# A two-block transformer kernel: score tiles, TensorE taps, norm sums, mask selects, band bias and key projection rearranged

## The chip, the cores and the metric

One Trainium2 chip, one core of it. The metric is the device time in microseconds (us) of one execution of the whole kernel; the kernel before took 2129.66 us as the median of three runs (2129.12 to 2134.75).

## What is computed

`reference` runs two transformer blocks on one sequence of 512 tokens, width 1024, all in float32. The parts that the change touches, cut to what matters:

```python
# first block: sliding-window attention beside a convolution branch
proj = rms_norm(h, mix_pre_g) @ w_in              # q (8 heads x 64), k, v (2 heads), u (2 x 512)
s = einsum(q, k) * scale + bias_by_distance       # blocks of 128 queries, 256 keys, window 128
p = softmax with a sink term;  attn_out = p @ v
a, gate = split(u);  c = a * sigmoid(gate)
c = depthwise causal convolution of c, width 31, 512 channels
c = silu(layer_norm(c)) @ w_conv_pw
h = h + rms_norm(concat(attn_out, c) @ w_out)
h = h + rms_norm((silu(hn @ w_gate) * (hn @ w_up)) @ w_down)
# second block: spatial gating beside attention on selected keys, then a table of experts
z = tril(spatial_w) @ layer_norm(gelu(v));  y_a = gelu(u) * z
k = rope(rms_norm(c_n @ w_uk)); vv = c_n @ w_uv;  q = rope(rms_norm(q))
y_b = softmax over the 256 (or fewer) keys with the highest index scores
h = h + merge(y_a, y_b) @ w_o;  h = h + peer(rms_norm(h))
```

## The kernel before

**Arithmetic.** Tokens lie in four blocks of 128 (`tb`). Large products are split: each float32 operand becomes a high part (a cast on ScalarE, ACT) and a low part (a subtraction on VectorE, DVE), and `mm3` (L155 to L158) makes three matmuls of them on TensorE (PE). A weight unit (`unit`, L132) is one load of 128 x 1024 on SP's queue, a cast on ACT (L138) and a subtraction on DVE (L140), in a ring of four; `next_unit` takes the units in the order in which they are packed. Plain float32 matmuls (transposes, scores, taps, means) show two records each in the trace. PSUM has eight banks, four with the tag "a" and four with "b".

**Order.** The program is traced by Tile, which gives each engine its own queue: of what is ready by its own estimate it issues first what was traced first, so the order of the code is a priority and not the exact order of a queue. Each queue then runs strictly in order on the chip. Work on different streams is interleaved by generators: `advance(gen, us)` traces as much of a generator as the given budget covers, `zipped` alternates several and `chain` puts them one behind the other. `tc.issue_after(x)` (`order`) queues an instruction behind `x` on the same engine without waiting for its end.

**First block, attention and convolution (L332 to L543).** `conv(c, ...)` makes one of four channel groups: a gated input `hc`, a first tap on ACT (L358), then the other 30 taps as multiply-adds of 128x512 on DVE (L368), each reading and writing `acc[c]`. For groups 2 and 3 the first `N_PE_TAPS[c]` taps (12 and 8) are instead matmuls on PE against diagonal matrices (`pe_taps`, L363; the diagonals are made on ACT, L347), and one DVE addition (L364) joins their sum to `acc[c]`. L498 to L500 trace both `pe_taps` ahead of the DVE taps of groups 2 and 3. Before the projections of q, k and v (L417), L401 to L407 build the band bias: four transfers on POOL's queue that read a small DRAM tile in reversed rows (L403), four matmuls (L405), four DVE additions (L406). `att1(b)` (L428) is the attention of block b: score matmuls (L435) and their DVE evacuation (L439) into two score tiles `sa`, of which the pool has `SA_BUFS` = 4 in all; maxima on DVE (L446), exponentials and scaling on ACT (L455, L460), transposes (L466) and products with v (L469) on PE, and a split into `cathi`/`catlo` (L472). Blocks 0 and 1 run together, then 2 and 3 (`att23`, L478), which at its step 3 (counted from 0) also traces the first two units of the output projection for token blocks 0 and 1 (L482 to L484). Behind all of it come the mean over channels (L513), the rest of those two units (L515, L533) between the steps of the layer norm (L516 to L538), and the pointwise convolution (L539).

**Transitions (`transition`, L243).** Three times the kernel ends a projection, adds it to `h`, normalises and transposes. Per token block: squares with a sum on ACT for each half (L253, L293), an addition of the two sums on DVE (L281, L295), scale and epsilon on DVE (L163), the power -1/2 on POOL (L164), products on DVE (L284, L298), transposes on PE (L183). The first two transitions do this twice per block (norm of the result, norm for the next layer), the third once.

**Second block (L602 to L862).** Index scores, then a top-k on DVE (`topk`, L704: 16 rounds of maximum and replacement for each of blocks 1 to 3), traced in small steps between the projections, with the attention `att2` chained behind it. The query projection goes to four "a" banks (L725 to L727). Then, for each block, six short matmuls project keys and values into a "b" bank (L743 to L746); ACT copies the values (L747) and squares queries and keys (L751, L752), DVE normalises (L755, L757, reading both banks), rotates, and PE makes one more projection into a "b" bank (L760) and transposes (`turn`). Then come the value projections (L822), the layer norm of the gate, two gates (L840) and the spatial gate (L843 to L855), which reads `wsT`. Its lower triangle is kept by four selects on POOL (L815 to L817), with no order given but their place in the code. Eight more gate projections follow among the steps of `att2`.

## Time and profile before

| | |
|---|---|
| runs, us | 2129.12, 2129.66, 2134.75 (median 2129.66) |
| profiled execution, us | 2132.12 |
| its span in the profile, us | 2130.4 |
| mean granted TensorE clock | 0.988 of full |
| first block, attention and convolution | about 34 to 200 us of the span |
| first, second, third transition | about 200 to 255, 584 to 627, 900 to 945 us |
| second block up to its merge | about 627 to 820 us |
| experts | from about 945 us to the end |

How to read the profile: it shows one execution; busy times are per engine, and a wait is put down to what ended it. PE is the matmul part of TensorE, PEld its weight load. A granted clock of 1.00 is 2.4 GHz; TensorE runs at that or at 1.2 GHz, so a value between is a mixture over the stretch. A wait of a row stands in brackets at its end, with the engine, tile and line that ended it. `x40` is the number of records in a row.

### The profile page before, as it was taken

The page shows a single profiled execution, that of the slowest core. Times are in us where ns is not written, and L with a number is a line of the kernel's source. Part 1 is how long each engine was busy: PE and PEld are TensorE (multiplying, and loading weights), DVE is VectorE, ACT ScalarE, POOL GpSimd, SP SyncE. Part 2 cuts the span into 40 slices and gives each one's busy share as a digit, 9 for nine tenths or more (in the row PEclk, how much of TensorE's full clock was granted, in tenths as well). Part 3 has the DMA queues.
Part 4 walks back from the last instruction along what each step waited for, and adds up shares of the span by engine and source line. Part 5 has one row for each costly group of instructions (what it writes and reads, how often), then busy time and mean ns, then how long its engine had stood idle before and what let it go on. Part 6 is the DMA issues. An engine that isn't in the chain of part 4 may idle for free.

```text
span 2130.4 us, 29554 instructions
## 1 busy us (share of the span) xinstructions
PE 2061.1 (97%) x11128; PEld 1753.5 (82%) x11128; DVE 1573.1 (74%) x2901; ACT 825.7 (39%) x1339; POOL 520.2 (24%) x383
## 2 busy tenths in 40 slices
PE   7989999999989999999999999999999999999999
PEld 6746888888877877888889899999888878788887
DVE  6974633332268955455699999998999988899997
ACT  5354422221244342333453455555433333333332
POOL 1000000000010000000032222220575656566573
PEclk9998999999999999999999999999999999999999
DMA  5202232333222222333278889899999999999995
GB/s 188 82 28 69 72 107 93 95 99 117 84 87 80 70 89 69 109 124 98 81 288 278 289 299 358 290 365 307 390 394 411 389 402 387 410 402 411 411 399 223
DMA packets 163281, 476.47 MB, mean 224 GB/s; under 512 B 13865, under 2 KB 57265, under 8 KB 161218
## 3 DMA queue, kind: packets, MB, share of 16 engines
...
## 4 chain that ended last, share of the span: by engine, by line
PE 54%; DVE 21%; issue 13%; DMA 8%; POOL 3%; ACT 2%; DVEq 0%; POOLq 0%; SPq 0%; ACTq 0%
PE bank_a L156 12%; PE bank_a L157 12%; PE bank_a L158 12%; DVE wlo L140 5%; PE bank_b L156 4%; PE bank_b L157 4%; PE bank_b L158 4%; DMA rows<-in_peer_u_dram,gidx 2%; DVE rows L957 2%; POOL rows L941 2%; DMA rows<-in_peer_v_dram,gidx 2%; DMA al<-a_dram 2%; DVE h L964 2%; DVE rows L949 2%; PE bank_b L1108 1%
## 5 line engine op out<-in xcount | busy, mean ns | idle before, releaser
L138 ACT CAST whi<-raw 128x1024 fp32r<-128x1024 f32 (+1 forms) x413 | 431.9, 1047 | 884.0 <-PE bank_a L157 332.0
L140 DVE TENSOR_TENSOR wlo<-raw,whi 128x1024 fp32r<-128x1024 f32 (+1 forms) x413 | 499.9, 1213 | 265.9 <-ACT whi L138 263.6
L156 PE MATMUL bank_a<-xhi,whi 128*128 128x320 f32 (+2 forms) x1600 | 549.3, 344 | 0.8 <-ACT xhi L152 0.8
L158 PE MATMUL bank_a<-xhi,wlo 128*128 128x320 f32 (+2 forms) x1600 | 546.2, 342 | 3.3 <-DVE wlo L140 3.3
L157 PE MATMUL bank_a<-xlo,whi 128*128 128x320 f32 (+2 forms) x1600 | 548.0, 343 | 0.6 <-DVE xlo L153 0.6
L941 POOL DMA_INDIRECT rows<-in_peer_u_dram,gidx x192 | 279.0, 1453 | 553.4 <-DVE gidx L1042 143.1
L158 PEld LDWEIGHTS bank_a<-xhi,wlo 128*128 128x128 f32 x1600 | 303.5, 190 | 31.6 <-DVE wlo L140 5.3
L156 PEld LDWEIGHTS bank_a<-xhi,whi 128*128 128x128 f32 x1600 | 302.8, 190 | 28.3 <-ACT xhi L152 1.8
L157 PEld LDWEIGHTS bank_a<-xlo,whi 128*128 128x128 f32 x1600 | 303.7, 190 | 26.9 <-DVE xlo L153 1.6
L941 POOL DMA_INDIRECT rows<-in_peer_v_dram,gidx x128 | 206.2, 1611 | 115.2 <-DVE h L964 91.2
L164 POOL TENSOR_TENSOR rstd<-rstd,neghalf 128x1 f32<-128x1 f32 (+2 forms) x37 | 25.2, 682 | 844.2 <-DVE rstd L163 832.4
L156 PE MATMUL bank_a<-whi,wvhi 128*128 128x512 f32 x512 | 201.9, 394 | 7.4 <-ACT wvhi L152 7.3
L157 PE MATMUL bank_a<-wlo,wvhi 128*128 128x512 f32 x512 | 202.0, 394 | 1.7 <-DVE wlo L140 1.6
L158 PE MATMUL bank_a<-whi,wvlo 128*128 128x512 f32 x512 | 201.7, 394 | 1.7 <-DVE wvlo L153 1.6
L964 DVE SCALAR_TENSOR_TENSOR h<-rows,ga,h 128x1024 f32<-128x1024 f32 x128 | 164.1, 1282 | 5.6 <-DMA rows<-in_peer_v_dram,gidx 4.2
L957 DVE SCALAR_TENSOR_TENSOR rows<-rows,h 128x1024 f32<-128x1024 f32 x128 | 152.8, 1220 | 9.9 <-DMA rows<-in_peer_u_dram,gidx 9.9
L156 PEld LDWEIGHTS bank_a<-whi,wvhi 128*128 128x128 f32 x512 | 97.0, 189 | 28.7 <-ACT wvhi L152 9.1
L158 PEld LDWEIGHTS bank_a<-whi,wvlo 128*128 128x128 f32 x512 | 97.2, 190 | 24.9 <-DVE wvlo L153 4.2
L157 PEld LDWEIGHTS bank_a<-wlo,wvhi 128*128 128x128 f32 x512 | 97.0, 189 | 21.6 <-DVE wlo L140 2.4
L156 PE MATMUL bank_b<-whi,wvhi 128*128 128x512 f32 x256 | 99.9, 390 | 0.0
L158 PE MATMUL bank_b<-whi,wvlo 128*128 128x512 f32 x256 | 99.6, 389 | 0.0
L157 PE MATMUL bank_b<-wlo,wvhi 128*128 128x512 f32 x256 | 99.6, 389 | 0.0
(403 smaller groups left out, 3272.5 us busy)
## 6 DMA issues: line engine op xcount, KB each, us to landing
...
raw<-in_ut_dram SPq DMA_DIRECT2D x128, 512.0 KB, 5.8
raw<-in_peer_v_dram SPq DMA_DIRECT2D x128, 512.0 KB, 8.0
...
```

The source lines that it names most:

```text
L138: lead[0] = S.copy(hi[:, :n], raw[:, :n]).ins
L140: pace[0] = V.tensor_tensor(lo[:, :n], raw[:, :n], hi[:, :n].bitcast(F32), op=OP.subtract).ins
L156: T.matmul(o, lh, rh, start=start, stop=False)
L157: T.matmul(o, lh, rl, start=False, stop=False)
L158: T.matmul(o, ll, rh, start=False, stop=stop)
L164: G.tensor_tensor(r, r, neghalf[:, :shape[1]], op=OP.pow)
L941: G.indirect_dma_start(out=r, out_offset=None, in_=table, in_offset=bass.IndirectOffsetOnAxis(ap=idx[:, k:k + 1], axis=0))
L949: V.scalar_tensor_tensor(r, r, 1.0, hn2, op0=OP.mult, op1=OP.mult, accum_out=ga2[:, k:k + 1])
L957: V.scalar_tensor_tensor(r, r, 1.0, hn3, op0=OP.mult, op1=OP.mult, accum_out=ga[:, k:k + 1])
L964: V.scalar_tensor_tensor(h[3], r, ga[:, k:k + 1], h[3], op0=OP.mult, op1=OP.add)
L1108: T.matmul(gp[:, j, :], o_[:, g2, :, t2], oh1[:, g2, :, t2], start=o_ is ohs[0], stop=o_ is ohs[-1])
```

## The change

Seven edits:

- `N_PE_TAPS` becomes (0, 0, 8, 8): four taps of group 2 go from PE to DVE, and four diagonals are no longer made. `SA_BUFS` becomes 7.
- The two `pe_taps` are traced inside `att23`, at its steps 4 and 6 (counted from 0), when all scores of blocks 2 and 3 are traced; the DVE taps of groups 2 and 3 that the budget has reached by then are traced ahead of them.
- The output projection's first two units are traced for all four token blocks behind the mean, one ahead of the variance and one behind the matmul that spreads the reciprocal root.
- The band bias is made in a function that is called behind projections 1 to 4 of the six.
- In the transitions, squares are scaled by 1/32 inside the activation, so that `rsqrt2` can add the two sums and epsilon in one DVE instruction.
- The key and value projection of block j is traced behind step j of the query projection, with the keys copied to SBUF on ACT (`ksb`), and the later steps read the copy.
- The four selects on `wsT` are issued behind the last power on POOL traced so far, that of the key norms.

```diff
--- before.py
+++ after.py
@@ -28,9 +28,9 @@
 GATHER = 0.5
 G_US = 2.3
 NSPILL = 100
-N_PE_TAPS = (0, 0, 12, 8)
+N_PE_TAPS = (0, 0, 8, 8)
 N_GATE = 5
-SA_BUFS = 4
+SA_BUFS = 7
 CONV_US = 4.4
 ATT_US = 2.0
 ATT2_US = 1.0
@@ -157,11 +157,20 @@
         T.matmul(o, lh, rl, start=False, stop=False)
         T.matmul(o, ll, rh, start=False, stop=stop)
 
+    rooted = [None]
+
     def rsqrt(ssq, scale, shape, after=None):
         r = small.tile(shape, F32, name="rstd", tag=f"rstd{shape[1]}")
         with order(after):
             V.tensor_scalar(r, ssq, scale, EPS, op0=OP.mult, op1=OP.add)
-        G.tensor_tensor(r, r, neghalf[:, :shape[1]], op=OP.pow)
+        rooted[0] = G.tensor_tensor(r, r, neghalf[:, :shape[1]], op=OP.pow).ins
+        return r
+
+    def rsqrt2(ssq):
+
+        r = small.tile([128, 1], F32, name="rstd", tag="rstd1")
+        V.tensor_scalar(r, ssq[:, 0:1], ssq[:, 1:2], EPS, op0=OP.add, op1=OP.add)
+        rooted[0] = G.tensor_tensor(r, r, neghalf[:, 0:1], op=OP.pow).ins
         return r
 
     def norm(wk, src, g_b, xs=None, after=(None, None)):
@@ -250,7 +259,7 @@
         ssq = [small.tile([128, 2], F32, name=f"ssqo{tb}", bufs=2) for tb in range(4)]
 
         def sumsq(o, tb, hf):
-            S.activation(xhi[:, tb, 4 * hf:4 * hf + 4, :], o.rearrange("p (k t) -> p k t", k=4), AF.Square,
+            S.activation(xhi[:, tb, 4 * hf:4 * hf + 4, :], o.rearrange("p (k t) -> p k t", k=4), AF.Square, scale=1.0 / 32,
                          accum_out=ssq[tb][:, hf:hf + 1])
 
         os0, j0 = pre or ([bank("a") for _ in range(4)], 0)
@@ -277,9 +286,7 @@
             if gp is not None:
                 sumsq(os1[tb], tb, 1)
                 V.tensor_tensor(xs[:, 512:], os1[tb], g_post[:, 512:], op=OP.mult)
-                s1 = small.tile([128, 1], F32, name="ssq1")
-                V.tensor_tensor(s1, ssq[tb][:, 0:1], ssq[tb][:, 1:2], op=OP.add)
-                r = rsqrt(s1, 1.0 / 1024, [128, 1])
+                r = rsqrt2(ssq[tb])
                 for sl in halves:
                     V.scalar_tensor_tensor(h[tb][:, sl], xs[:, sl], r, h[tb][:, sl], op0=OP.mult, op1=OP.add)
             else:
@@ -290,10 +297,8 @@
 
             sq = small.tile([128, 2], F32, name="ssqn", bufs=2)
             for hf, sl in enumerate(halves):
-                S.activation(xs[:, sl], h[tb][:, sl], AF.Square, accum_out=sq[:, hf:hf + 1])
-            s1 = small.tile([128, 1], F32, name="ssq1")
-            V.tensor_tensor(s1, sq[:, 0:1], sq[:, 1:2], op=OP.add)
-            r = rsqrt(s1, 1.0 / 1024, [128, 1])
+                S.activation(xs[:, sl], h[tb][:, sl], AF.Square, scale=1.0 / 32, accum_out=sq[:, hf:hf + 1])
+            r = rsqrt2(sq)
             for sl in halves:
                 V.scalar_tensor_tensor(xs[:, sl], h[tb][:, sl], r, g_next[:, sl], op0=OP.mult, op1=OP.mult)
             last = xs
@@ -398,16 +403,14 @@
         bap = bdr[:, :]
         band = cst1[:, 0:256]
         flip = cst1[:, 256:384]
-        for j in range(4):
+
+        def band_bias(j):
             rev = pt_.tile([128, 2, 256], F32, name="rev", bufs=2)
             nc.gpsimd.dma_start(rev, bass.AP(tensor=bap.tensor, offset=bap.offset + 2 * j * 383, ap=[[1, 128], [383, 2], [1, 256]]))
             fp = bank("b")
             T.matmul(fp, flip, rev.rearrange("p a k -> p (a k)"), start=True, stop=True)
             V.tensor_tensor(bias[:, 2 * j:2 * j + 2, :], fp.rearrange("p (a k) -> p a k", a=2),
                             band[:, None, :].to_broadcast([128, 2, 256]), op=OP.add)
-
-        stt.close()
-        at = pool("b1at", stack=st, side="right")
 
 
         qT = pa.tile([128, 4, 512], F32, name="qT")
@@ -418,7 +421,11 @@
             S.copy(dst, proj_T(next_unit(), xhi, xlo))
             if n_ in (0, 1):
                 diagonals(2 + n_)
+            if 1 <= n_ <= 4:
+                band_bias(n_ - 1)
             d = advance(cv, d + CONV_US)
+        stt.close()
+        at = pool("b1at", stack=st, side="right")
         vps = bank("b")
         for b in range(4):
             T.transpose(vps[:, b * 128:(b + 1) * 128], vT[:, b * 128:(b + 1) * 128], ident)
@@ -472,21 +479,17 @@
             split(cathi[:, b, 0:4, :], catlo[:, b, 0:4, :], op_.rearrange("p (c t) -> p c t", c=4))
             yield 0.7
 
-        os0, us0 = [], []
-        src1 = (lambda tb, k: cathi[:, tb, k, :]), (lambda tb, k: catlo[:, tb, k, :])
+        c23 = []
 
         def att23():
 
             for n_, t in enumerate(zipped(att1(2), att1(3))):
-                if n_ == 3:
-                    us0.extend(next_unit() for _ in range(2))
-                    os0.extend(bank("a") for _ in range(2))
-                    proj_tok(os0, *src1, range(2), 8, 0, us0, 2, 512)
+                if n_ in (4, 6):
+                    c23[n_ // 2 - 2][1]()
                 yield t
 
         av = chain(zipped(att1(0), att1(1)), att23())
         da = 0.0
-        c23 = []
         for c in (2, 3):
             oa = proj_T(next_unit(), xhi, xlo)
             d = advance(cv, d + CONV_US)
@@ -495,11 +498,7 @@
             c23.append(conv(c, oa, og))
             d = advance(cv, d + CONV_US)
             da = advance(av, da + ATT_US)
-        for c in (0, 1):
-            c23[c][1]()
-            da = advance(av, da + ATT_US)
-        c23 = [c_[0] for c_ in c23]
-        cv = chain(cv, zipped(*c23))
+        cv = chain(cv, zipped(*[c_[0] for c_ in c23]))
         while True:
             n1 = next(cv, None)
             da = advance(av, da + ATT2_US)
@@ -511,8 +510,9 @@
         mu = bank("b")
         for c in range(4):
             T.matmul(mu, oneD, acc[c], start=(c == 0), stop=(c == 3))
-        os0.extend(bank("a") for _ in range(2))
-        proj_tok(os0, *src1, (2, 3), 8, 0, us0[:1], 2, 512)
+        src1 = (lambda tb, k: cathi[:, tb, k, :]), (lambda tb, k: catlo[:, tb, k, :])
+        os0 = [bank("a") for _ in range(4)]
+        proj_tok(os0, *src1, range(4), 8, 0, [next_unit()], 2, 512)
         var = bank("b")
         for c in range(4):
             V.tensor_tensor(acc[c], acc[c], mu, op=OP.subtract)
@@ -530,7 +530,7 @@
             V.tensor_scalar(rdg[:, tb, :], ident, r4[:, tb:tb + 1], None, op0=OP.mult)
         rs = bank("b")
         T.matmul(rs, ones, rdg.rearrange("p b t -> p (b t)"), start=True, stop=True)
-        proj_tok(os0, *src1, (2, 3), 8, 2, us0[1:], 2, 512)
+        proj_tok(os0, *src1, range(4), 8, 2, [next_unit()], 2, 512)
         for c in range(4):
             V.tensor_tensor(acc[c], acc[c], rs, op=OP.mult)
             sl = wk.tile([128, 512], F32, name="sg", bufs=2)
@@ -723,10 +723,17 @@
     ukv = next_unit(512)
     uTs = [gts[:, 2 * N_GATE - 4 + g, :] for g in range(4)]
     qb = [bank("a") for _ in range(4)]
+    ksb = wk.tile([128, 4, 128], F32, name="ksb")
     for j in range(4):
         proj_tok(qb, chi, clo, range(4), 8, 2 * j, [next_unit()], 2, 512)
         if j == 0:
             index_block(3)
+        kv = bank("b")
+        for k in range(2):
+            mm3(kv[:, :256], cnhi[:, j, k], cnlo[:, j, k], ukv[0][:, k * 256:(k + 1) * 256],
+                ukv[1][:, k * 256:(k + 1) * 256], k == 0, k == 1)
+        S.copy(vv[:, j, :], kv[:, 128:256])
+        S.copy(ksb[:, j, :], kv[:, :128])
         d = advance(tk, d + TOPK_US)
 
     def turn(tb, qk):
@@ -740,21 +747,16 @@
 
     qk_ = None
     for tb in range(4):
-        kv = bank("b")
-        for k in range(2):
-            mm3(kv[:, :256], cnhi[:, tb, k], cnlo[:, tb, k], ukv[0][:, k * 256:(k + 1) * 256],
-                ukv[1][:, k * 256:(k + 1) * 256], k == 0, k == 1)
-        S.copy(vv[:, tb, :], kv[:, 128:256])
         qk = wk.tile([128, 5, 128], F32, name="qk", bufs=2)
         s5 = small.tile([128, 5], F32, name="s5")
         for hh in range(4):
             S.activation(qk[:, hh, :], qb[tb][:, hh * 128:(hh + 1) * 128], AF.Square, accum_out=s5[:, hh:hh + 1])
-        S.activation(qk[:, 4, :], kv[:, :128], AF.Square, accum_out=s5[:, 4:5])
+        S.activation(qk[:, 4, :], ksb[:, tb, :], AF.Square, accum_out=s5[:, 4:5])
         r = rsqrt(s5, 1.0 / 128, [128, 5])
         for hh in range(4):
             V.scalar_tensor_tensor(qk[:, hh, :], qb[tb][:, hh * 128:(hh + 1) * 128], r[:, hh:hh + 1], qkg[:, 0:128],
                                    op0=OP.mult, op1=OP.mult)
-        V.scalar_tensor_tensor(qk[:, 4, :], kv[:, :128], r[:, 4:5], qkg[:, 128:256], op0=OP.mult, op1=OP.mult)
+        V.scalar_tensor_tensor(qk[:, 4, :], ksb[:, tb, :], r[:, 4:5], qkg[:, 128:256], op0=OP.mult, op1=OP.mult)
         rope(qk, tb, 0, 16, 5)
 
         S.activation(uTs[tb], proj_T(next_unit(), xhi, xlo, o=bank("b")), AF.Gelu_apprx_tanh)
@@ -812,9 +814,10 @@
     vb = bcast_row(wk, A["gsm"], 1024, 512, "vb")
     wsT = wk.tile([128, 4, 128], F32, name="wsT")
     nc.scalar.dma_start(wsT, A["wsT"])
-    for g in range(4):
-        G.affine_select(out=wsT[:, g, :], in_=wsT[:, g, :], pattern=[[1, 128]], compare_op=OP.is_ge,
-                        fill=0.0, base=0, channel_multiplier=-1)
+    with order(rooted[0]):
+        for g in range(4):
+            G.affine_select(out=wsT[:, g, :], in_=wsT[:, g, :], pattern=[[1, 128]], compare_op=OP.is_ge,
+                            fill=0.0, base=0, channel_multiplier=-1)
     bs = wk.tile([1, 512], F32, name="bs")
     nc.scalar.dma_start(bs, A["spatial_b"])
     vbk = [bank("a") for _ in range(4)]
```

## Rows read from the trace of the kernel before

**Rows 1.** Busy time, share of the span and instructions of PE (page, part 1).

```profile
PE 2061.1 (97%) x11128; PEld 1753.5 (82%) x11128; DVE 1573.1 (74%) x2901; ACT 825.7 (39%) x1339; POOL 520.2 (24%) x383
```

**Rows 2.** PE's waits, whole span: us in total, times, longest us.

```profile
PE bank_b L183 <- DVE xs L298: 7.3, 6, 3.3
...
PE bank_b L156 <- DVE qk L757: 4.4, 1, 4.4
```

**Rows 3.** Windows, first block: stretch, length, busy PE, PEld, DVE, ACT, POOL, clock, DMA, GB/s.

```profile
34.50:162.80 128.30, 118.62 (x493) 80.30 (x492) 110.80 (x189) 58.28 (x155) 3.43 (x5) 0.98 0.20 63
105.50:119.00 13.50, 13.50 (x39) 7.17 (x39) 3.73 (x7) 11.84 (x37) 0.00 (x0) 1.00 0.19 46
132.10:162.80 30.70, 23.84 (x102) 14.04 (x101) 28.45 (x58) 18.79 (x62) 0.00 (x0) 0.91 0.00 1
139.90:145.70 5.80, 5.80 (x25) 4.40 (x24) 5.80 (x13) 0.12 (x1) 0.00 (x0) 1.00 0.00 0
171.50:187.30 15.80, 11.22 (x58) 8.23 (x57) 7.76 (x16) 7.92 (x12) 1.03 (x1) 0.80 0.12 33
```

**Rows 4.** DVE's waits, 34.5 to 162.8 us.

```profile
DVE den L457 <- ACT sa L455: 6.3, 3, 4.0
...
DVE bias L406 <- PE bank_b L405: 3.1, 3, 1.7
DVE sa L439 <- PE bank_b L435: 2.4, 2, 1.3
...
DVE acc L368 <- ACT acc L358: 0.9, 1, 0.9
```

**Rows 5.** PE in order of time, first block: start us, us, engine, line.

```profile
108.52 17.34 PE L363 MATMUL bank_b<-hc,dgs 128*128 128x512 f32 x40
...
169.50 1.98 PE L513 MATMUL bank_b<-acc,oneD 128*128 128x512 f32 x4
```

**Rows 6.** DVE in order of time, convolution taps.

```profile
59.72 11.35 DVE L368 SCALAR_TENSOR_TENSOR acc<-hc,cw,acc 128x512 f32<-128x512 f32 x17
...
160.47 2.33 DVE L368 SCALAR_TENSOR_TENSOR acc<-hc,cw,acc 128x512 f32<-128x512 f32 x3
```

**Rows 7.** DVE in order of time, a norm in the first transition.

```profile
221.74 0.16 DVE L295 TENSOR_TENSOR ssq<-ssqn 128x1 f32<-128x1 f32 x1 [0.79 <-ACT xs L293]
221.94 0.15 DVE L163 TENSOR_SCALAR rstd<-ssq 128x1 f32<-128x1 f32 x1
222.82 1.41 DVE L298 SCALAR_TENSOR_TENSOR xs<-h,rstd,g_next 128x512 f32<-128x512 f32 x2 [0.73 <-POOL rstd L164]
```

**Rows 8.** DVE in order of time, second transition.

```profile
607.63 1.05 DVE L140 TENSOR_TENSOR wlo<-raw,whi 128x870 fp32r<-128x870 f32 x1
...
619.89 0.15 DVE L163 TENSOR_SCALAR rstd<-ssq 128x1 f32<-128x1 f32 x1
623.91 1.42 DVE L298 SCALAR_TENSOR_TENSOR xs<-h,rstd,g_next 128x512 f32<-128x512 f32 x2 [3.87 <-POOL rstd L164]
```

**Rows 9.** POOL in order of time, second transition.

```profile
607.85 1.24 POOL L164 TENSOR_TENSOR rstd<-rstd,neghalf 128x1 f32<-128x1 f32 x1 [4.35 <-DVE rstd L163]
...
622.33 1.03 POOL L816 TENSOR_SCALAR_AFFINE_SELECT wsT<-wsT 128x128 f32<-128x128 f32 x4 [4.87 <-DMA wsT<-in_wsT_dram]
```

**Rows 10.** PE in order of time, second transition and key projection.

```profile
624.81 1.94 PE L183 MATMUL bank_b<-cst,xs 128*128 128x128 f32 x8 [3.30 <-DVE xs L298]
...
691.41 0.55 PE L156 MATMUL bank_b<-whi,cnhi 128*128 128x256 f32 x1 [4.41 <-DVE qk L757]
```

**Rows 11.** Windows, second block (columns as in rows 3).

```profile
626.00:640.00 14.00, 14.00 (x100) 13.62 (x99) 7.98 (x25) 6.33 (x16) 1.70 (x4) 0.93 0.33 114
691.40:708.00 16.60, 16.59 (x72) 13.62 (x72) 14.77 (x46) 6.77 (x28) 2.33 (x2) 0.85 0.21 63
660.00:750.00 90.00, 85.11 (x389) 69.70 (x387) 84.79 (x210) 32.84 (x82) 7.57 (x9) 0.96 0.26 82
```

**Rows 12.** ACT in order of time, the copy of one block's values.

```profile
675.12 0.25 ACT L747 COPY vv<-bank_b 128x128 f32<-128x128 f32 x1
```

## The prediction

> **What bounds the kernel now.** The page comes first: TensorE (PE) is busy 97% of the span [rows 1], so time comes off only where PE stands still, runs at the lower clock, or waits in a way that stops everything. The list of PE's waits over the whole execution says where that is [rows 2]: transposes wait for a normalised block (7.3 us in six waits, one of them 3.3), and one wait of 4.4 us stands at the key projection. The change also edits the first 190 us, where waits are short but work is badly placed, so I read that stage by windows [rows 3]. Between 34.5 and 162.8, while the convolution taps run, VectorE (DVE) is busy 110.80 of 128.30 us: it is nearly full, and its 17.5 us of idle time lie in one place above all, 105.5 to 119.0, where it works 3.73 us of 13.5. DVE's waits name the reasons [rows 4]: 6.3 us behind the exponentials, 3.1 behind the band-bias matmuls, 2.4 behind scores, 0.9 behind a start on ScalarE (ACT). In 105.5 to 119 the taps of channel group 2 could have run, but they are queued behind the sum of that group's TensorE taps, and these run late in one block of 20 [rows 5]. The last DVE tap starts about 162 [rows 6]; the mean's matmuls wait still longer, for the attention of blocks 2 and 3, whose scores came only when the four score tiles were free, and end at 171.5 [rows 5].
>
> **Part A: score tiles, taps, band bias, output projection.** I cost these together, since they share one bound: DVE's ledger from 34.5 on.
> Removed from DVE's idle time: with seven tiles, three of the four for blocks 2 and 3 exist at once, so their scores can follow the last projection without waiting for the transposes of blocks 0 and 1. Sixteen TensorE taps follow them, at 17.34/20 = 0.87 us each (two records a matmul, [rows 5]), 13.9 us in place of 17.3. The DVE taps of groups 2 and 3 are now issued ahead of the sums with the TensorE taps, so DVE always has some to do.
> Added to DVE: four taps at 11.35/17 = 0.67 us [rows 6], 2.7 us, and two low-part subtractions of the attention output that used to come after 162.8, bounded by one tap's price, 1.3 together. So 110.8 + 2.7 + 1.3 = 114.8.
> Idle time that stays: 0.9 for the first start, 1.3 for the first scores (the longest wait in that row, no tap is ready then) [rows 4], and a loss like that of 132.1 to 162.8, where taps were at hand and DVE still lost 30.70 - 28.45 = 2.3 us [rows 3]. Together 4.5. The last tap then ends at 34.5 + 114.8 + 4.5 = 153.8, and the last mean matmul 1.0 us later (half of the 1.98 us row [rows 5]), 154.8 instead of 171.5: **16.7 us**.
> The band bias is inside this sum. Its four transfers on POOL's queue, eight matmul records and four additions all remain. They move behind projections 1 to 4, and the 3.1 us that DVE lost to them [rows 4] become tap time. PE no longer stands in front of a transfer; a transfer that is late now would have to be so by a whole projection.
> The output projection of blocks 0 and 1 (24 matmuls, 5.8 us [rows 3]) moves from before the mean to behind it, with its two weight loads on SP's queue, their casts on ACT and subtractions on DVE. The stretch from the mean to the pointwise convolution, 171.5 to 187.3, has PE busy 11.22 of 15.8 us at a granted clock of 0.80. The same work at full clock is about 9 us, and 9 + 5.8 = 14.8 still fits: I cost it at nothing. Without that cover it costs at most 5.8. The two subtractions land on a DVE that works 7.76 us of that stretch.
> Bounds of A: upwards, if no loss but the 2.2 us of the two starts stays, 19.0, and if the low clock in the stretch goes as well, 0.2 x 15.8 = 3.2 more, 22.2. Downwards, if the attention of blocks 2 and 3 still ends 8.7 us behind the last tap as now, 162.8 - 153.8 = 9.0, less 1.2 us by which 11.22 + 5.8 exceeds the stretch: 7.8. I take 16.7, since the scores start earlier by at least the 17.34 us of the tap block that stands in front of them now.
>
> **Part B: one addition less in each norm.** The chain is addition, scale, power, product: 221.74, 221.94, 222.82 [rows 7]. The addition's row is 0.16 us, and there are two on the way to each transpose in the first two transitions (16), one in the third (4). PE waits for these products six times, all in the first two transitions [rows 2]. Without the long one (Part C) that is five waits of at most 0.3 us each to win, 1.6; some additions lie beside other DVE work, and then nothing is won. I take half, **0.8**, bounds 0 and 1.6. The changed scaling sits inside activations that exist already.
>
> **Part C: masks behind the norms.** In the second transition the scale of the last block is done at 619.89, but its product starts at 623.91 [rows 8]. Between them POOL runs four selects on the spatial weights at 622.33, having stood 4.87 us in front of them for their transfer, with the power queued behind [rows 9]. PE starts the transposes at 624.81 after 3.30 us [rows 10]. With the power first, the product follows the scale by 0.88 us as in [rows 7]: 623.91 - 620.77 = 3.1 us earlier. After the wait the clock is 0.93 for 14 us [rows 11], worth up to 1.0; I take half. **3.6**, bounds 2.0 and 4.2. The selects (1.03 us for the four) now follow the last power of the key norms on POOL. In the code their reader, the spatial gate, comes only after the value projections and two gates, and the next power after the value projections; that is their cover. Without it they would cost their 1.0.
> By the Trainium skill (SBUF — State Buffer, Who interferes with whom), a GpSimd instruction that reads SBUF and a VectorE instruction with two SBUF inputs exclude each other for a whole instruction. The trace bears that out: one power took 1.24 us [rows 9] while DVE ran a subtraction of two SBUF inputs [rows 8]. It speaks against the new place, where DVE is almost full; by that rule the selects could take 1.0 us from Part D.
>
> **Part D: keys beside projections.** The third key projection waits 4.41 us for a PSUM bank that DVE still reads [rows 10], and then the clock is 0.85 for 16.6 us [rows 11], worth 2.5: together 6.9. The 24 short matmuls stay, four steps earlier, and the bank is freed by copies: four more of about 0.25 us [rows 12] on ACT, which is busy 32.84 of 90 us there. A late one costs its own length. What is late next is DVE's top-k: in 660 to 750 DVE is idle 90 - 84.79 = 5.2 us [rows 11], so it can follow PE by 5.2 at best. PE has gate projections to do meanwhile. Bounds 1.0 (top-k makes PE wait at the next bank) and 6.9; I take the middle, **4.0**.
>
> **Sum.** 16.7 + 0.8 + 3.6 + 4.0 = 25.1 us. The profiled execution took 2132.1 us around its span of 2130.4, so it would take 2107.0. The median of the runs is 2.5 lower than it, so the median forecast is **2104.5**. Nothing behind 1000 us is edited, and I expect it to shift as a whole.
>
> **The rivals.** First, attention stays last. Scores start early but the chain over DVE maxima, ACT exponentials and transposes ends after the taps. For it: PE has 13.9 us of taps queued between the scores and those transposes. Against: ACT has room. Part A is then 7.8 and the time 2113.4. Chance 0.15.
> Second, top-k becomes the bound: Part D and Part B give nothing, 2109.3. For it: DVE is at 94% in 660 to 750. Against: ten gate projections of 24 matmuls (5.8 us for 24 [rows 3]) need no mask. Chance 0.10.
> Third, the tiles do nothing: scores of blocks 2 and 3 are held by the four PSUM banks instead, as two stay taken while the eighth tile is missing. Only the 3.1 us of the band bias are left of A: 2118.1. Chance 0.05.
> Fourth, the other side: **the sixteen taps come too late.** On DVE 28 of the 44 taps and two sums stand behind them, 28 x 0.67 + 1.3 = 20.1 us. The forecast of 153.8 holds while the TensorE taps end by 133.7. Every microsecond later costs one, and from 158.8 on the kernel is slower than now. If they ran behind all of the attention as it ends now, about 169.5, the time would be 2104.5 + 35.8 = 2140.3. Against it: they need only the scores ahead of them. Chance 0.04.
>
> **How the numbers follow.** The forecast has 0.63; 0.03 is left for gains that cancel to within 0.3%, which is about what a measurement of this kernel can tell from no change. Faster by over 0.3%: 0.63 + 0.15 + 0.10 + 0.05 = 0.93; slower 0.04. All lower bounds together give 10.8 us, all upper ones 34.9. That all four fall to one side is unlikely; the range runs from 13.5 to 32.5 us won, **2097 to 2116**, with the first two rivals inside.
>
> **What would show it.** Right: hardly any DVE idle time between the last projections and the last tap; scores of blocks 2 and 3 directly behind the projections with the taps next; the mean's matmuls ending near 155; no wait of PE for band-bias transfers or at the key projection; selects on POOL behind the key norms. Wrong: an idle stretch on DVE in front of the sums with TensorE taps, mean matmuls waiting for attention, or new PE waits for top-k masks between 700 and 760.

## The result, and the profile after

Five runs of the changed kernel took 2110.11 to 2117.52 us, median **2110.99**; the kernel before took 2129.66 in the same session. The ratio is 0.9917, 95% interval 0.9896 to 0.9938. The forecast was 2104.5, with a range of 2097 to 2116: faster, and inside the range, but 18.7 us won instead of 25.1. (Three of the five runs took 2110.1 to 2111.0 at a mean granted clock of 0.991 to 0.992, and two took 2116.8 to 2117.5, beyond the range, at 0.988 to 0.989; only the first was profiled, so whether those two had the low clock of experiments 1 and 2 is not shown.) The profiled execution took 2110.99 around a span of 2109.3.

The total hides where the time went, so I take the same TensorE instruction in both traces at each stage and compare its start:

| start of, us | before | after | won so far |
|---|---|---|---|
| first scores of the first block | 88.81 | 85.74 | 3.1 |
| pointwise convolution | 187.32 | 176.35 | 11.0 |
| last transposes of the first transition | 251.93 | 240.46 | 11.5 |
| first transposes of the second transition | 595.84 | 584.10 | 11.7 |
| last index scores, second block | 656.90 | 639.58 | 17.3 |
| first matmul of the spatial gate | 741.44 | 726.44 | 15.0 |
| last product with v, second block | 816.49 | 801.02 | 15.5 |
| third-last matmul of the experts' tables | 1484.76 | 1468.24 | 16.5 |
| end of the span | 2130.4 | 2109.3 | 21.1 |

So Part A gave 11.0 (forecast 16.7), Parts B and C together 6.3 (forecast 4.4), the key stage took 1.9 back up to the last product with v (forecast +4.0 for Part D), and 5.6 came behind it, where only the sums of the third transition were edited (with the old sums put back, experiment 2, it takes 667.4 us from the last product with v to the tables, in the changed kernel 667.2). Of these 5.6, 2.5 are the amount by which the profiled execution of before lies above its median.

The page answers to [rows 1]: TensorE is still busy 97%, with 10 us less of work.

```profile
PE 2050.9 (97%) x11120; PEld 1747.3 (83%) x11120; DVE 1573.4 (75%) x2885; ACT 826.6 (39%) x1339; POOL 527.7 (25%) x383
```

TensorE's waits over the whole span (us in total, times, longest), beside [rows 2]:

```profile
PE bank_b L742 <- DVE qk L629: 7.4, 2, 5.3
...
PE bank_b L192 <- DVE xs L303: 2.7, 5, 0.7
```

The waits for a normalised block fell from 7.3 to 2.7 and lost their long one. The wait at the key projection is gone, and a larger one, 7.4 us, stands at the turns of queries and keys, where there was none of that size.

The windows of the first block (columns as in [rows 3]), up to the last tap and from the layer norm's first subtraction to the pointwise convolution:

```profile
34.50:158.80 124.30, 120.94 (x498) 79.65 (x498) 114.03 (x195) 60.10 (x157) 3.43 (x5) 1.00 0.21 65
105.50:115.00 9.50, 6.95 (x29) 3.10 (x28) 8.40 (x16) 9.44 (x30) 0.00 (x0) 1.00 0.15 56
115.00:125.00 10.00, 9.50 (x43) 4.68 (x42) 6.98 (x12) 3.62 (x6) 0.00 (x0) 1.00 0.17 52
125.00:138.80 13.80, 13.80 (x34) 6.06 (x33) 13.66 (x33) 9.01 (x34) 0.00 (x0) 1.00 0.14 39
138.80:158.80 20.00, 19.69 (x77) 10.22 (x76) 16.09 (x27) 10.99 (x30) 0.00 (x0) 1.00 0.00 1
161.80:176.40 14.60, 9.94 (x54) 7.11 (x52) 6.62 (x16) 7.04 (x11) 1.03 (x1) 0.82 0.11 36
```

VectorE worked 114.03 us, as forecast (114.8), but stood still for 10.3 instead of 4.5: 4.1 between 105.5 and 125, 3.9 between 138.8 and 158.8, 2.1 before 105.5. And TensorE, which was full in 105.5 to 119 before [rows 3], now works 6.95 of 9.5 us there. TensorE in order of time says why:

```profile
107.39 1.93 PE L476 MATMUL bank_a<-pT,vt 128*64 128x512 f32 x4 [0.59 <-ACT pT L475]
...
113.82 0.44 PE L473 MATMUL bank_b<-cst,sa 128*128 128x128 f32 x2 [1.02 <-ACT sa L467]
114.18 0.70 PE L442 MATMUL bank_b<-kT,qT 64*128 64x256 f32 x2
...
124.96 14.00 PE L368 MATMUL bank_b<-hc,dgs 128*128 128x512 f32 x32
```

The scores of blocks 2 and 3 (L442) did not follow the projections at 105.4. They stand behind transposes and products of blocks 0 and 1, which wait for ScalarE, and start at 114.18; the sixteen taps run from 124.96 to 138.96. VectorE in order of time at the end of the taps:

```profile
151.85 0.69 DVE L153 TENSOR_TENSOR catlo<-bank_a,cathi 128x512 fp32r<-128x512 f32 x1 [1.94 <-ACT cathi L152]
154.28 0.69 DVE L153 TENSOR_TENSOR catlo<-bank_a,cathi 128x512 fp32r<-128x512 f32 x1 [1.74 <-ACT cathi L152]
154.88 3.89 DVE L373 SCALAR_TENSOR_TENSOR acc<-hc,cw,acc 128x512 f32<-128x512 f32 x5
160.68 1.23 DVE L140 TENSOR_TENSOR wlo<-raw,whi 128x1024 fp32r<-128x1024 f32 x1 [1.90 <-ACT whi L138]
```

Two low-part subtractions of blocks 2 and 3 stand in front of the last five taps and wait for the attention; then a weight unit that nobody needs yet stands in front of the layer norm, which starts at 161.82. GpSimd in the second transition and at the key norms, beside [rows 9]:

```profile
605.52 0.55 POOL L173 TENSOR_TENSOR rstd<-rstd,neghalf 128x1 f32<-128x1 f32 x1 [3.35 <-DVE rstd L172]
...
688.60 1.03 POOL L819 TENSOR_SCALAR_AFFINE_SELECT wsT<-wsT 128x128 f32<-128x128 f32 x4
```

The last power comes without the selects in front of it; they run at 688.60. The new waits at the turns, TensorE in order of time, beside [rows 10]:

```profile
684.74 0.63 PE L742 MATMUL bank_b<-cst,qk 128*128 128x128 f32 x4 [2.14 <-DVE qk L629]
691.90 1.09 PE L742 MATMUL bank_b<-cst,qk 128*128 128x128 f32 x4 [5.27 <-DVE qk L629]
```

And the window behind the second of them (columns as above), beside [rows 11]:

```profile
691.90:708.00 16.10, 16.09 (x64) 13.29 (x65) 13.96 (x27) 2.86 (x4) 0.00 (x0) 0.85 0.24 67
```

The same low clock of 0.85 follows the wait as before. VectorE reaches the third norm at 680.0, 10.7 us behind the rotation of the second, and the fourth at 687.2.

### The profile page after: what moved, and what is told of

It reads as the page before. It is cut to its first block, busy times and chain, and to the rows that moved or that the text cites. A ratio compares the mean times of both kernels' runs of the same rounds, so it can differ in the third digit from the quotient of the medians.

```text
span 2109.3 us, 29516 instructions
## 1 busy us (share of the span) xinstructions
PE 2050.9 (97%) x11120; PEld 1747.3 (83%) x11120; DVE 1573.4 (75%) x2885; ACT 826.6 (39%) x1339; POOL 527.7 (25%) x383
## 4 chain that ended last, share of the span: by engine, by line
PE 62%; DVE 17%; issue 12%; DMA 5%; POOL 2%; ACT 2%; DVEq 0%; POOLq 0%; SPq 0%; ACTq 0%; another core or an unknown queue 0%
PE bank_a L156 14%; PE bank_a L157 14%; PE bank_a L158 14%; PE bank_b L156 5%; PE bank_b L157 5%; PE bank_b L158 5%; DVE wlo L140 4%; DMA rows<-in_peer_u_dram,gidx 2%; DMA al<-a_dram 2%; POOL rows L944 2%; DVE rows L952 2%; DVE rows L960 2%; PE bank_b L1111 1%; DVE mask L710 1%; DMA rows<-in_peer_v_dram,gidx 1%
## 5 line engine op out<-in xcount | busy, mean ns | idle before, releaser
L944 POOL DMA_INDIRECT rows<-in_peer_u_dram,gidx x192 | 284.1, 1480 | 546.3 <-DVE gidx L1045 144.4
L173 POOL TENSOR_TENSOR rstd<-rstd,neghalf 128x1 f32<-128x1 f32 x20 | 13.9, 695 | 616.2 <-DVE rstd L172 616.2
```

The costliest lines, as they stand in the source:

```text
L173: rooted[0] = G.tensor_tensor(r, r, neghalf[:, 0:1], op=OP.pow).ins
L944: G.indirect_dma_start(out=r, out_offset=None, in_=table, in_offset=bass.IndirectOffsetOnAxis(ap=idx[:, k:k + 1], axis=0))
```

## The experiments

Eleven kernels ran. The table has the median (in brackets the interval of the ratio to the kernel before), the granted clock of the window 115 to 125, and the start of five of the instructions above in the profiled execution. Experiments start from the changed kernel unless they say otherwise.

| kernel | median, us | clock | pointwise | index scores | spatial gate | last v | tables |
|---|---|---|---|---|---|---|---|
| before | 2129.66 | 1.00 | 187.32 | 656.90 | 741.44 | 816.49 | 1484.76 |
| after | 2110.99 (0.9896-0.9938) | 1.00 | 176.35 | 639.58 | 726.44 | 801.02 | 1468.24 |
| keys_back | 2116.41 (0.9927-0.9953) | 1.00 | 176.50 | 639.65 | 724.55 | 799.64 | 1468.23 |
| sums_back | 2119.11 (0.9934-0.9960) | 0.50 | 180.59 | 647.18 | 734.15 | 808.71 | 1476.08 |
| masks_back | 2116.57 (0.9914-0.9944) | 0.50 | 181.29 | 644.74 | 731.47 | 806.03 | 1473.16 |
| lows_behind | 2114.68 (0.9912-0.9938) | 0.66 | 177.32 | 639.60 | 725.97 | 800.53 | 1467.28 |
| taps_early | 2113.56 (0.9902-0.9929) | 1.00 | 177.75 | 641.47 | 728.62 | 803.20 | 1470.87 |
| qk4 | 2117.03 (0.9904-0.9939) | 0.50 | 181.18 | 644.59 | 723.05 | 805.89 | 1473.19 |
| mean_split | 2114.09 (0.9901-0.9929) | 0.50 | 179.07 | 641.56 | 728.01 | 802.56 | 1469.33 |
| tiles4 (one run) | 2114.67 | 0.83 | 177.18 | 640.08 | 726.75 | 801.30 | 1470.80 |
| mean_first | 2115.01 (0.9913-0.9937) | 0.83 | 176.52 | 638.99 | 725.99 | 800.56 | 1470.47 |
| scores_mean_first | **2104.16** (0.9869-0.9901) | 1.00 | 169.13 | 629.97 | 716.87 | 791.45 | 1458.68 |
| best_keys_back | 2106.03 (0.9857-0.9893) | 1.00 | 169.17 | 630.00 | 715.03 | 790.12 | 1458.34 |

The first thing to learn from it is how to read it. From the tables to the end of the span the thirteen profiles took 640.3 to 646.5 us, although the queues of TensorE, VectorE, ScalarE and GpSimd hold the same instructions in the same order there. (The three kernels with the keys in their old place, before, keys_back and best_keys_back, are among the four longest, 645.6 to 646.5; one profile each can't tell that from chance.) And a clock of 0.50 in the clock column goes with a pointwise convolution that starts up to 5 us later. Medians of single runs can't tell edits of 2 us apart here. Stretches between two landmarks can: from the end of the first transition to the second's first transposes all kernels took 343.64 or 343.65, and the two with the old sums 343.91.

**1. Masks left without an order** (masks_back).

```diff
-    with order(rooted[0]):
+    with order(None):
         for g in range(4):
             G.affine_select(out=wsT[:, g, :], in_=wsT[:, g, :], ...
```

> The changed kernel with the four selects on the spatial weights left without an order, as before. Theory: they stand in GpSimd's queue in front of the last power of the second transition again and wait for their transfer, so the last transposes of that transition wait 3.3 us again and the clock behind them falls for a while: 3.8 us slower, about 2114.8. Rival: the product is late for another reason (VectorE's own queue), and the selects' place is worth nothing: 2111.0.

From the last transposes of the first transition to the last index scores it took 399.34 us, the changed kernel 399.12, the kernel before 404.97. The rival's number holds, 0.2 us, but not its reason. GpSimd in order of time:

```profile
610.44 0.55 POOL L173 TENSOR_TENSOR rstd<-rstd,neghalf 128x1 f32<-128x1 f32 x1 [3.36 <-DVE rstd L172]
612.86 1.04 POOL L819 TENSOR_SCALAR_AFFINE_SELECT wsT<-wsT 128x128 f32<-128x128 f32 x4 [1.87 <-DMA wsT<-in_wsT_dram]
613.86 1.07 POOL L166 TENSOR_TENSOR rstd<-rstd,neghalf 128x1 f32<-128x1 f32 x2
```

The selects are not in front of the last power though nobody ordered them; that the scheduler takes the power for ready first because each norm has one addition less is likely, but not shown. Two edits remove the same stall, and either is enough. The profiled run, 2117.50, was longer than the changed kernel's for another reason, the window 115 to 125:

```profile
115.00:125.00 10.00, 10.00 (x18) 3.17 (x18) 3.31 (x6) 2.40 (x4) 0.00 (x0) 0.50 0.17 52
```

The queues up to there are those of the changed kernel, and the window before shows the same work (6.96 of 9.5 us); yet TensorE ran at 1.2 GHz for ten microseconds, and the pointwise convolution started 4.9 us later.

**2. Sums added apart again** (sums_back).

```diff
-                r = rsqrt2(ssq[tb])
+                s1 = small.tile([128, 1], F32, name="ssq1")
+                V.tensor_tensor(s1, ssq[tb][:, 0:1], ssq[tb][:, 1:2], op=OP.add)
+                r = rsqrt(s1, 1.0 / 1024, [128, 1])
```

> The changed kernel with the two norm sums added in an instruction of their own again in all three transitions, the squares unscaled. Theory: that edit is worth more than forecast, since each of TensorE's waits for a normalised block ends with this chain: 0.5 us in the first transition and about 2 in the second, so about 2113.5, with TensorE's waits for normalised blocks near 5 us instead of 2.7. Rival: it is worth the forecast 0.8 and the rest of the second transition's gain came with the masks: about 2111.8.

The same stretch took 401.31: the masks' order alone wins 404.97 - 401.31 = 3.7 us, and the sums on top of it 2.2. In the first transition (pointwise convolution to last transposes) it took 65.28 against 64.11 in masks_back, whose clock was as low: 1.2 more. So with the masks' order in place the sums are worth another 3.4, four times the forecast and more than this theory's 2.5. The theory is right that they count at TensorE's waits; the profiled run, 2120.76, again has the low clock of 115 to 125 in it.

**3. Keys put back** (keys_back).

```diff
     for j in range(4):
         proj_tok(qb, chi, clo, range(4), 8, 2 * j, [next_unit()], 2, 512)
...
-        kv = bank("b")
-        for k in range(2):
-            mm3(kv[:, :256], cnhi[:, j, k], cnlo[:, j, k], ...
-        S.copy(vv[:, j, :], kv[:, 128:256])
-        S.copy(ksb[:, j, :], kv[:, :128])
...
     for tb in range(4):
+        kv = bank("b")
+        for k in range(2):
+            mm3(kv[:, :256], cnhi[:, tb, k], cnlo[:, tb, k], ...
+        S.copy(vv[:, tb, :], kv[:, 128:256])
```

> The changed kernel with the key and value projections put back behind the query projection, each in front of its block's norm (the keys are read from PSUM again); all else as changed. Theory: in this stage VectorE is full (top-k between the norms), so the four turns come when VectorE reaches them, and the 24 short matmuls were only filling TensorE's waits there. From the end of the index scores to the first spatial-gate matmul the kernel before took 82.6 us and the changed one 84.9, so putting them back should win 2.3: about 2108.7, with the waits at the turns (7.4 us in two) falling to about 5, most of it at a key projection as before. Rival: the move was worth the 4.0 of the forecast and the new wait has another cause (the top-k is less far along because the stage starts earlier); then the kernel gets slower, about 2115.

The old wait is back, to the tenth (TensorE's waits, 640 to 830):

```profile
PE bank_b L156 <- DVE qk L757: 4.4, 1, 4.4
PE bank_b L735 <- DVE qk L629: 0.5, 1, 0.5
PE bank_b L846 <- DVE sa L784: 0.5, 1, 0.5
```

From the index scores to the spatial gate it took 84.90 us (changed 86.86, before 84.54), to the last product with v 159.99 (161.44, 159.59). Theory right in this stage: the moved keys cost 1.5 to 2.0 there, and TensorE's waits are 5.4 us instead of 7.4. The median, 2116.41, is near the rival's 2115, but not by the rival's reason, since the stage got shorter. From the last product with v to the tables the order with the keys put back took 668.6 us (before 668.3) and the changed one 667.2, so at the tables the two are level. The traces show where: up to about 1043 us, 240 us behind that product, all thirteen profiles agree to 0.13 us, and by about 1116 us they lie 0.4 under to 2.7 over the changed kernel, those with the moved keys too. TensorE's queue is the same in all of them there, so these 1.4 us are within the spread of the experts' stretch. The difference of the medians lies behind the tables (646.5 us against 641.1).

**4. Four tiles for queries and keys** (qk4).

```diff
-        qk = wk.tile([128, 5, 128], F32, name="qk", bufs=2)
+        qk = wk.tile([128, 5, 128], F32, name="qk", bufs=4)
```

> The changed kernel with four tiles instead of two for the normalised queries and keys. Theory: the third and fourth norm wait for a tile until the first and second have been turned, and that puts them behind four rounds of top-k on VectorE; this is the wait at the turns (7.4 us in two) that took the place of the one at the key projection. With four tiles the norms follow each other, the waits vanish, and the first spatial-gate matmul comes 7 to 9 us earlier after the index scores (86.9 us in the changed kernel, 84.9 with the keys put back). What is late next is the top-k, about 733, which the gate projections cover; about 2104 if all of it reaches the end. Rival: VectorE as a whole is the bound of this stage (its top-k ends at 733 either way), the wait only moves to the spatial gate or to the attention behind the top-k, and at most 2 us are won.

The spatial gate comes 78.46 us behind the index scores instead of 86.86, so the theory of the wait holds: the third norm stood behind the tile ring, with five rounds of top-k and four weight subtractions in the 10.7 us in front of it. But the last product with v comes at 161.30, the changed kernel's 161.44. TensorE's longest wait from 640 to 830, and the window from the gate to the last product with v, in the changed kernel and in this one:

```profile
PE bank_b L851 <- DVE gv L838: 4.4, 2, 3.0
...
726.44:801.02 74.58, 74.45 (x325) 53.45 (x325) 41.63 (x74) 32.01 (x67) 0.00 (x0) 1.00 0.23 71
...
723.05:805.89 82.84, 78.26 (x325) 55.85 (x325) 46.97 (x85) 32.01 (x67) 0.58 (x2) 0.94 0.20 64
```

TensorE gets to the spatial gate early and waits for VectorE there; from gate to last v it takes 82.84 us instead of 74.58, at a granted clock of 0.94 instead of 1.00. The rival is right about the sum, but its reason, VectorE as the bound of the whole stage, is not shown. The top-k ends 90.2 us behind the index scores instead of 93.9, and still nothing is won: from there to the last product with v TensorE works 71.0 of 71.1 us (67.4 of 67.5 in the changed kernel), VectorE about half of them. What the runs show is that the wait returned where the two engines next met, with a lower clock behind it.

**5. Four score tiles** (tiles4).

```diff
-SA_BUFS = 7
+SA_BUFS = 4
```

> The changed kernel with four score tiles instead of seven; the queues of all engines keep the same order. Theory: the scores of blocks 2 and 3 come at 114 to 125 only because the queue has them behind the transposes of blocks 0 and 1, and by then the old tiles are free: no score waits for a tile, and the TensorE taps start within 1 us of the changed kernel (124.96 at full clock). This is the third rival of the prediction as far as the tiles go. Other side: the tiles let the scores run between those transposes; with four the scores wait, and the taps start 3 us or more later.

Taps start at 126.73, with a clock of 0.83 in 115 to 125. The kernel mean_first below, with seven tiles, the same queues up to here and the same 0.83, starts them at 126.56. TensorE's and VectorE's waits from 104 to 128 are the same in both, item by item. The tiles do nothing in this order; the third rival of the prediction was right about them, though not about the time, and that PSUM banks are the reason is not shown.

**6. Low parts behind the last tap** (lows_behind).

```diff
-            split(cathi[:, b, 0:4, :], catlo[:, b, 0:4, :], op_.rearrange("p (c t) -> p c t", c=4))
+            o4 = op_.rearrange("p (c t) -> p c t", c=4)
+            if b < 2:
+                split(cathi[:, b, 0:4, :], catlo[:, b, 0:4, :], o4)
+            else:
+                S.copy(cathi[:, b, 0:4, :], o4)
+                lows.append((b, o4))
...
+        with order(tapped[0]):
+            for b, o4 in lows:
+                V.tensor_tensor(catlo[:, b, 0:4, :], o4, cathi[:, b, 0:4, :].bitcast(F32), op=OP.subtract)
```

> The changed kernel with the two low-part subtractions of attention blocks 2 and 3 queued behind the last convolution tap on VectorE instead of in front of its last five. Theory: VectorE stood still 1.94 and 1.74 us in front of these two because they wait for the attention; without that, and with the two (1.4 us) behind it, the last tap ends about 153.7 instead of 158.8, which is the end that the forecast gave, and the layer norm's subtraction starts about 155.6 instead of 161.8. The 24 output-projection matmuls that ran in front of it then run inside the layer norm. If the norm's stretch (14.5 us, TensorE at work 9.9 of them at a clock of 0.82) takes them in, 5 to 6 us are won: about 2105.5. Rival: the stretch is already as full as it can be, each moved matmul lengthens it, and at most 1 us is won: 2110.

VectorE in order of time:

```profile
147.27 9.55 DVE L374 SCALAR_TENSOR_TENSOR acc<-hc,cw,acc 128x512 f32<-128x512 f32 x13
156.74 1.28 DVE L518 TENSOR_TENSOR catlo<-bank_a,cathi 128x512 fp32r<-128x512 f32 x2
162.47 2.48 DVE L527 TENSOR_TENSOR acc<-acc,bank_b 128x512 f32<-128x512 f32 x4 [4.46 <-PE bank_b L521]
```

The clock fell in this execution too and the TensorE taps began 3.0 us later, yet the last tap ended at 156.8, 2.0 earlier. That half of the theory holds. But then VectorE waits 4.46 for the last mean matmul, which TensorE has queued behind twenty projection matmuls and runs at 161.41. A transfer of the bottleneck, not a gain: the pointwise convolution came at 177.32.

**7. The mean ahead of the projection** (mean_split, then mean_first; both on lows_behind).

```diff
+        u0 = next_unit()
+        proj_tok(os0, *src1, range(2), 8, 0, [u0], 2, 512)
+        for c in range(4):
+            meaned = T.matmul(mu, oneD, acc[c], start=(c == 0), stop=(c == 3)).ins
+        with order(meaned):
+            proj_tok(os0, *src1, (2, 3), 8, 0, [u0], 2, 512)
```

> The kernel with the two low-part subtractions behind the last tap, and in addition the first unit of the output projection split around the mean: token blocks 0 and 1 in front of its last matmul, 2 and 3 queued behind it. Theory: with the subtractions moved alone, the last tap ended 2.0 us earlier although the TensorE taps began 3.0 later, but the last mean matmul still stood behind 20 or more projection matmuls (4.5 us of VectorE idle). With 12 in front the mean ends about 1 us behind the last tap, so from the start of the TensorE taps to the pointwise convolution it takes about 46 us instead of 51.4 (changed kernel) and 49.4 (subtractions alone). Rival: the projection matmuls are then missing in front of the mean and lengthen the layer norm instead; 49 us or more.

From the taps' start to the pointwise convolution it took 49.8 us, not 46: the rival. All four mean matmuls slid behind the first twelve projection matmuls, and the last of them behind some more. The second version holds them in front:

```diff
+        meaned = [T.matmul(mu, oneD, acc[c], start=(c == 0), stop=(c == 3)).ins for c in range(4)]
+        with order(meaned[2]):
+            proj_tok(os0, *src1, [0], 8, 0, [u0], 2, 512)
+        with order(meaned[3]):
+            proj_tok(os0, *src1, range(1, 4), 8, 0, [u0], 2, 512)
```

> As the kernel with the split mean, but the first three mean matmuls and the last one are now each held in front of the projection matmuls behind them, so that the last mean matmul has only a few of these ahead of it (in the split version all four mean matmuls had slid behind 12 of them, and the last one ended 5.8 us behind the last tap). Theory: the layer norm's subtraction then starts at most 2 us behind the last tap; the pointwise convolution starts 17 to 18 us behind the last tap instead of 20.7, about 175.5 if the clock falls in 115 to 125 as in the split version's profile (179.1) and about 171 if it doesn't. Rival: the projection matmuls that fall into the layer norm lengthen it by their own 4 us; 178 or more with the fall.

The last tap ended at 155.4, the subtraction started at 159.6 (4.2 behind, not 2), and the pointwise convolution at 176.5, 21 behind the tap. Missed: what no longer ran in front of the norm ran inside it. By these edits behind the taps alone nothing was won.

**8. Group 2's taps in their old place** (taps_early).

```diff
-                if n_ in (4, 6):
-                    c23[n_ // 2 - 2][1]()
+                if n_ == 6:
+                    c23[1][1]()
...
+        c23[0][1]()
         cv = chain(cv, zipped(*[c_[0] for c_ in c23]))
```

> The changed kernel with the eight TensorE taps of channel group 2 traced right behind the projections again, in front of the transposes of attention blocks 0 and 1; group 3's eight stay behind the scores. Theory: in the changed kernel TensorE worked only 6.95 of the 9.5 us from 105.5 to 115, because the taps that filled this place before had been moved behind the scores; after those waits the granted clock of 115 to 125 was 1.00 in two of five profiled executions, 0.66 in one and 0.50 in two, and the two cost 4 to 5 us up to the pointwise convolution. With eight taps there the waits vanish and the clock stays at 1.00; the pointwise convolution starts about 175 in every execution, and the median is 3 to 4 us under the mean of executions with and without the fall, about 2109. Rival: the fall has nothing to do with these waits; then the clock of 115 to 125 is below 1.00 here too in some profile, and the time stays about 2113.

The clock of 115 to 125 stayed at 1.00, and its six runs lay between 2111.5 and 2115.4. But the convolution started at 177.75, not 175: the taps push the scores of blocks 2 and 3 to 118, and the waits come later (TensorE in order of time):

```profile
124.40 2.83 PE L442 MATMUL bank_b<-kT,qT 64*128 64x256 f32 x16 [1.26 <-DVE sa L446]
...
137.55 3.54 PE L473 MATMUL bank_b<-cst,sa 128*128 128x128 f32 x16 [3.06 <-ACT sa L467]
```

And the clock falls there, in the window of the second of these waits:

```profile
135.00:145.00 10.00, 7.45 (x23) 3.10 (x24) 9.67 (x23) 8.82 (x30) 0.00 (x0) 0.83 0.00 1
```

**9. Scores first, as the forecast had them** (scores_mean_first, on mean_first).

```diff
+        def att():
+            a01, a23 = zipped(att1(0), att1(1)), zipped(att1(2), att1(3))
+            for _ in range(6):
+                yield next(a01)
+            while len(c23) < 2:
+                yield 0.0
+            for _ in range(4):
+                yield next(a23)
+            for c in (0, 1):
+                c23[c][1]()
+            yield from a01
+            yield from a23
...
-            sas = [at.tile([128, 4, 256], F32, name="sa", bufs=SA_BUFS) for _ in range(2)]
+            sas = [at.tile([128, 4, 256], F32, name="sa", bufs=6) if b else at.tile([128, 4, 128], F32, name="sa0", bufs=2) for _ in range(2)]
```

> As the kernel with the mean held in front, and in addition the scores of attention blocks 2 and 3 traced right behind the last projection, with the sixteen TensorE taps next and the transposes of blocks 0 and 1 behind these; block 0 gets two tiles of half the size, so that all eight score tiles exist at once in the space of seven. Theory: this is the order that the forecast took for granted. TensorE then has no wait between 105 and 125, so the granted clock stays at 1.00 there in every execution; VectorE always has scores or taps to do, so it idles at most 2.5 us from 105 on, and the last tap ends at 34.5 + 112.7 of work + 2.1 + 2.5 = 151.8 (forecast 153.8, changed kernel 158.8). The pointwise convolution starts about 169.5 instead of 176.4, and the median comes to about 2105. Rival: attention as a whole, now behind the taps, ends last (all transposes and products of four blocks, 17 us and more behind 126), the mean waits for nothing but the projection has no attention output ready, and the pointwise convolution starts no earlier than 174.

TensorE in order of time, at the end of the projections:

```profile
104.52 2.00 PE L444 MATMUL bank_b<-kT,qT 64*128 64x256 f32 x16
107.41 3.58 PE L444 MATMUL bank_b<-kT,qT 64*128 64x256 f32 x16 [0.89 <-DVE sa L448]
111.12 14.00 PE L369 MATMUL bank_b<-hc,dgs 128*128 128x512 f32 x32
```

The windows up to the last tap, and the two behind the projections:

```profile
34.50:151.70 117.20, 114.14 (x479) 75.22 (x477) 110.66 (x193) 58.84 (x154) 3.43 (x5) 1.00 0.22 68
105.50:115.00 9.50, 8.34 (x35) 4.32 (x32) 8.93 (x19) 5.03 (x18) 0.00 (x0) 1.00 0.16 62
115.00:125.00 10.00, 10.00 (x25) 4.33 (x24) 10.00 (x26) 10.00 (x37) 0.00 (x0) 1.00 0.07 26
```

VectorE in order of time, at the end of the taps:

```profile
137.08 14.60 DVE L374 SCALAR_TENSOR_TENSOR acc<-hc,cw,acc 128x512 f32<-128x512 f32 x21
151.59 1.28 DVE L525 TENSOR_TENSOR catlo<-bank_a,cathi 128x512 fp32r<-128x512 f32 x2
152.89 2.48 DVE L537 TENSOR_TENSOR acc<-acc,bank_b 128x512 f32<-128x512 f32 x4
```

Scores at 104.5, taps until 125, VectorE busy all ten microseconds of 115 to 125 and idle 6.5 us in all instead of 10.3, the last tap at 151.7 (expected 151.8), the layer norm at 152.9, the pointwise convolution at 169.1 (expected 169.5), 18.2 us earlier than in the kernel before. That the last tap came within 0.1 us of the expected is partly luck: VectorE worked 110.7 us instead of 112.7 and idled 6.5 instead of 4.6, and TensorE did wait, 1.2 of the 9.5 us from 105.5. The median, 2104.16, is under both kernels; its interval (0.9869 to 0.9901) just touches the changed kernel's (0.9896 to 0.9938). The scores' order alone, without the edits of experiments 6 and 7, was not run.

**10. The same with the keys put back** (best_keys_back; the edit of experiment 3).

> The last kernel (scores and taps first, mean in front) with the keys put back behind the query projection as before the change. Theory: from the index scores to the end of the second block's attention the changed order took 161.4 to 161.5 us, the old one 159.6 and 160.0, so 1.4 to 1.9 us are won there; in the run with the keys put back alone, the way from there to the first expert tables was 1.2 us longer, which I take for the spread of that part. If so the median is about 2102.5. Rival: the spread is no spread but the order of the later queues, the 1.2 us are lost again, and the median stays at 2104.

Again 1.8 us won at the spatial gate and 1.3 at the last v, again all but 0.3 of it gone at the tables, and 2106.03 for the median: the rival's number. Its reason, the order of the later queues, is not borne out: behind the last product with v every compute engine has the same instructions in the same order in both kernels, and the loss arises in the stretch of the experts that spreads (experiment 3). For the whole kernel the place of the key projection makes no difference that can be told.

## Why the prediction was right or wrong

**Faster, and the size.** Stage by stage: 11.0 (A) + 6.3 (B, C) - 1.9 (key stage) + 1.1 (last v to tables) + 2.1 (tables to the end, 4.6 in the spans less 2.5) = 18.6, for the 18.7 measured. Forecast: 16.7 + 4.4 + 4.0 = 25.1. "I expect it to shift as a whole" held only to within the spread of that last part, which alone can move the median by 2 or 3 us. The range held with some luck: without the 3.2 us of these last two stages, which no edit explains, 15.4 would be left, 2114.3, and the profiled run, which is the median, had the clock at 1.00 in 115 to 125.

**Part A, where the forecast failed.** Most terms were right. The band bias gave its 3.1 us (scores at 85.74 instead of 88.81; no run put it back alone, but TensorE's waits for its transfers between 34.5 and 106, below, have no counterpart after the change). The sixteen taps took 14.0 us (forecast 13.9). VectorE's work was 114.03 (114.8).

```profile
PE bank_b L405 <- DMA rev<-bdr: 2.7, 2, 1.5
```

The nothing for the output projection came out by luck: the norm's stretch took 14.5 us instead of 15.8, but 31 of the 48 matmuls of the two units still ran ahead of it (25 before). Where 35 and 40 ran inside, in mean_first and scores_mean_first, it took 16.9 and 16.2 us at a granted clock of 1.00.

Part A fell short by 5.7: the last tap came 5.0 us after the forecast (158.8 instead of 153.8), the norm began 3.0 behind it instead of 1.0 (a weight subtraction stands in front of it, and 22 projection matmuls in front of the last mean matmul), and its stretch gave 1.3 back. The step that failed is "their scores can follow the last projection without waiting for the transposes of blocks 0 and 1". Tiles were not what held them in this order: with four they come as soon (experiment 5). They are traced behind the attention of blocks 0 and 1, and TensorE's queue keeps that order, with its waits for ScalarE. So the attention of blocks 2 and 3 came late as well, and VectorE's idle time was 10.3 us instead of 4.5: 4.1 between 105.5 and 125, and 3.7 in front of the two low-part subtractions, to which the forecast gave their work of 1.3 but no wait. With the order put right, VectorE's last tap came at 151.7, 2 us ahead of the forecast (1.3 of them because the two subtractions then stand behind it), and the convolution 18.2 us earlier. Experiment 9 has this, an eighth score tile and the order of experiments 6 and 7 together; the latter alone brought nothing, and its profile had a clock of 0.83 in 115 to 125, so part of its distance to experiment 9 can be the clock.

What I costed at nothing and should not have: the twelve and eight taps of before were TensorE's cover for the softmax of blocks 0 and 1 (13.50 of 13.50 us busy [rows 3]). Moved behind the scores, they left 6.95 of 9.5, and the clock there then differs from one execution to the next: of nine profiles with this order, two stayed at 1.00, two show 0.83, one 0.66 and four 0.50. In the three of the last four that have the same queues up to the convolution it starts 4.2 to 4.9 us later. So Part A is 11.0 in the profiled execution, which is also the median run, and by these three about 6.5 where the clock is 0.50.

**The first and fourth rivals.** Attention did not stay last; its last product ended at 153.6, in front of the last tap. The fourth rival's condition, taps on TensorE that end past 133.7, came true: they ended at 138.96, 5.3 us later, and the last tap came 5.0 late. But the two are not linked as the rival has it: VectorE worked 13.66 of the 13.80 us up to 138.8, on maxima of the attention and on taps, and none of its waits is for a sum.

**Parts B and C.** C was right in place and size: 3.7 alone, forecast 3.6. B was mis-sized, 3.4 on top of C instead of 0.8, and above its bound of 1.6. I counted one addition of 0.3 us at each of five waits, but two lie on the way to each transpose, and in both transitions the transposes of the second to the fourth block came 1.1 to 2.6 us earlier than with the old sums (counted from the convolution, and from the end of the first transition). That B alone also removes C's stall no step foresaw: with B in place the order adds 0.2 (experiment 1). (The two make 7.1 and not 6.3, because from the convolution to the end of the first transition the kernel with the old sums took 65.3 us, the kernel before 64.6; no run says why.)

**Part D.** The step that failed is the choice of the middle between the bounds. The wait of 4.41 us at a PSUM bank turned up at the turns when the bank was no longer in the way, and at the spatial gate when the turns got their tiles (experiment 4). VectorE is late at each of these places, which is near the second rival's mechanism, but it does not bound the whole stage, since behind the top-k TensorE works without a gap. Without the 24 matmuls TensorE only waited longer at the turns, 7.4 us instead of 5.4 in the stage, and the clock behind the wait was 0.85 as before. The price lay outside the bounds, -1.9 instead of 1.0 to 6.9 (-1.5 by experiment 3), because I allowed top-k to make TensorE wait "at the next bank" but not for more than the old wait. The second rival's "B gives nothing" was wrong.

By the Trainium skill (SBUF — State Buffer, Who interferes with whom), a GpSimd instruction that reads SBUF, as the selects do, and a VectorE instruction with two SBUF inputs exclude each other. The forecast feared 1.0 us from that. The selects took 1.03 us at 688.60, as before, beside VectorE products that read PSUM and took their usual 1.12. No run here shows the exclusion at this place.
